# A hybrid attention and recurrence block: small-tile preparation beside attention, then a scan with batched solves beside the gates

## The chip, the core and the metric

The kernel runs on one core of one Trainium2 chip. The metric is the device time of one execution in microseconds; of several runs the median counts. One execution was taken by the hardware profiler; its span and rows are what is read below.

## What is computed

One layer over L = 1040 tokens (1024 and 16 meta tokens) of width 1024, batch 1, float32:

```python
hn = rms_norm(h, norm_mix)
q, k, v, f_logit, rw, gates = split(hn @ w_in)            # 3 x 512, 8, 1792, 2048
o_fox = forgetting attention: softmax(rms(q).rms(k)/8 + fcum[t] - fcum[s]) v, 8 heads of 64, causal
z = rw + mu * (shift(rw) - rw)                             # r, kr, vr: 512 each; zw, za, zg: 64, 64, 128
decay, a_rate, g = low-rank projections of zw, za, zg      # tanh, sigmoid
kk = kr * k_k / norm(kr * k_k)                             # per head
S_t = S_{t-1} diag(w_t) + (S_{t-1} a_t) b_t^T + v_t k_t^T; y_t = S_t r_t     # a = -kk, b = kk * a_rate
o_rwkv = (group_norm(y) + bonus) * g
merged = sigmoid(gates_1) * (o_fox @ w_bf) + sigmoid(gates_2) * (o_rwkv @ w_br)
h = h + merged @ w_o
h = h + (silu(conv(u_gate)) * conv(u_val)) @ ffn_down,  u = rms_norm(h, norm_ffn) @ ffn_up
```

The recurrence is computed in 17 chunks of 64 tokens. Within a chunk, the coupling of a token to the earlier ones is a strictly lower triangular 64 x 64 matrix a head, and (1 - A) has to be inverted: this inversion is called a solve here.

## The kernel before

All tensors lie with channels on partitions and tokens along the free axis. Large products run in three passes: weights and operands are split into float32r high and low parts, and `mm3` (L201 to L203) issues for each 128 x 128 weight tile the triple wh·xh, wh·xl, wl·xh. `wload` (L177) loads weights from DRAM through SP's queue (L185), rounds the high part on ACT (L188) and subtracts on POOL (L189). Small products are single float32 ones, for which the profile counts two passes each. Names: `mm`, `aux`, `tp`, `ch`, `gate`, `gn`, `t`, `s`, `o`, `rp` are PSUM tiles; names with `_d` lie in DRAM. Engines run in the order in which the program emits instructions, after a scheduler has interleaved the streams; DMAs issued on SP wait in SP's one queue.

Stage 1 (`stage1`, L259) does the first norm, in three chunks of tokens, then for each of four head pairs the preparation of the recurrence at the full width of 1040 tokens: projections (`rw_tile`), low-rank products (L304 to L313), cumulative decays, products `am` of a chunk's keys and queries (L394, stored to am_d L397), copies of the 32 x 32 diagonal blocks of these from DRAM to DRAM (`diags`, L404: a_d<-am_d, four a pair, runs of 128 bytes), transposes `bkt` (L411 to L415), and others. Stage 2 (`stage2`, L878) merges attention (`attention`, `q_block`) with the recurrence: `rw_pre` (L434) solves the systems of two chunks at a time, nine batches of 31 steps with two DVE operations each (L449, L451), `rw_chain` (L501) runs the 17 chunks, and `group_norm` (L847) follows at the end. The gates' projections, 384 triples, are a reserve: `fill` (L839) emits one to four triples at places where PE would wait, 84 of its steps right after stage 1. Stages 3 to 5 are the branches under the gates, the output projection with the second norm, and the MLP. `merge_streams` emits the steps of several generators in the order of virtual times that the `yield`s state.

```python
for k in range(2):                                   # diags, L401 to L404
    r = slice(32 * k, 32 * k + 32)
    for h in (2 * p, 2 * p + 1):
        nc.sync.dma_start(out=S.a_d[:, k, h], in_=S.am_d[:, r, h, r])
```

Of the kernel before, what the change touches and what calls it, by code (L numbers as in the profile page):

```python
# [7 lines left out]
F32 = mybir.dt.float32  # L8
F32R = mybir.dt.float32r
BF16 = mybir.dt.bfloat16  # L10
AF = mybir.ActivationFunctionType
# [26 lines left out]
CH = [(0, 346), (346, 692), (692, 1040)]  # L38
# [15 lines left out]
def constants(S):  # L54
    """The constants that the first products need."""
    nc, A, cp = S.nc, S.A, S.cp
    par = cp.tile([P, NPAR], F32, name="par")
    nc.sync.dma_start(out=par[:], in_=A["par"])
    S.par = lambda name, i=0: par[:, _PCOLS[name][0] + i:_PCOLS[name][0] + i + 1]
    S.pr = lambda name: par[:, _PCOLS[name][0]:_PCOLS[name][0] + _PCOLS[name][1]]  # L60
    S.ident = cp.tile([P, P], F32, name="ident")
    nc.sync.dma_start(out=S.ident[:], in_=A["ident"])
    S.ones = cp.tile([P, P], F32, name="ones")
    nc.vector.memset(S.ones[:], 1.0 / D)
    S.eps = cp.tile([P, 1], F32, name="eps")
    nc.vector.memset(S.eps[:], NORM_EPS)
    S.geps = cp.tile([P, 1], F32, name="geps")
    nc.vector.memset(S.geps[:], GN_EPS)
    S.wc = cp.tile([P, NCH, 4], F32, name="wc")


def constants2(S):
# [9 lines left out]
    S.a0h = lin("a0", 4, 0.5, 0.0)  # L82
    S.kah = lin("k_a", 4, 0.5, 0.0)
# [17 lines left out]
def stage0(S, p0):  # L101
    nc, tc = S.nc, S.tc
    S.w0 = []
# [7 lines left out]
    def tiles(*tags):  # L111
        r = []
        for t in tags:
            m = 6 if t[1:] in ("r_t", "k_t") else 3
            r.append(p0.tile([P, m, 348], F32, name="xt", tag=t))
        return r, [(i, j) for i, t in enumerate(r) for j in range(t.shape[1])][:KD]

    xs = []
    for c, (t0, t1) in enumerate(CH):
        n = t1 - t0  # L120
        tl, at = tiles(*(("zr", "zv", "sw"), ("tha", "inv", "ex"), ("ar_t", "cs"))[c])
        k = 0
        for t in tl:
            for j in range(0, t.shape[1], 3):
                m = min(3, KD - k)
                nc.sync.dma_start(out=t[:, j:j + m, :n], in_=S.A["xT"][:, k:k + m, t0:t1])
                k += m
                if k == KD:
                    break
        xs.append([tl[i][:, j] for i, j in at])  # L130
        if c == 0:
            constants(S)
        S.w0.append(wload(S, S.A["w_rw"][c], KD) if c < 2 else wload(S, S.A["w_rw"][c], KD, S.gp, "g", 1, 2))
    constants2(S)

    def stats(c):
        """1 / rms of a chunk's tokens, the same on all partitions."""
        n = CH[c][1] - CH[c][0]
        xt = xs[c]
        tl, at = tiles("bk_t", "kk")  # L140
        sq = [tl[i][:, j, :n] for i, j in at]
        na = 2
        for k in range(KD):
            with tc.issue_after(S.xhi[k].ins) if c == 1 else nullcontext():
                nc.scalar.activation(out=sq[k], in_=xt[k][:, :n], func=AF.Square)
                if k >= na:
                    nc.vector.tensor_tensor(out=sq[k % na], in0=sq[k % na], in1=sq[k], op=ALU.add)
        ps = psum(S, "aux")
        blk = [(0, 116), (116, 116), (n - 116, 116)]
        for j, (a, m) in enumerate(blk):  # L150
            for k in range(na):
                nc.tensor.matmul(ps[:m, j:j + 1], lhsT=sq[k][:, a:a + m], rhs=S.ones[:, 0:1], start=k == 0, stop=k == na - 1)
        r = p0.tile([P, 3], F32, name="r", bufs=2)
        nc.scalar.activation(out=r[:116], in_=ps[:116, 0:3], func=AF.Sqrt, bias=S.eps[:116])
        nc.vector.reciprocal(out=r[:116], in_=r[:116])
        ps = psum(S, "tp")
        for j, (a, m) in enumerate(blk):
            nc.tensor.matmul(ps[:, a:a + m], lhsT=r[:m, j:j + 1].broadcast_to([m, P]), rhs=S.ident[:m, :m], start=True, stop=True)
        return ps

    pss = [stats(0)]
    for c, (t0, t1) in enumerate(CH):
        ps = pss[c]
        n = t1 - t0
        xt = xs[c]
        for k in range(KD):
            nc.vector.scalar_tensor_tensor(out=xt[k][:, :n], in0=xt[k][:, :n], scalar=S.par("norm_mix", k),
                                           in1=ps[:, :n], op0=ALU.mult, op1=ALU.mult)
            S.xhi[k] = nc.scalar.copy(out=S.xh[k][:, 2 + t0:2 + t1], in_=xt[k][:, :n])  # L169
            nc.gpsimd.tensor_tensor(out=S.xl[k][:, 2 + t0:2 + t1], in0=xt[k][:, :n],  # L170
                                    in1=S.xh[k][:, 2 + t0:2 + t1], op=ALU.subtract)
        if c == 0:
            pss += [stats(1), stats(2)]
        yield c


def wload(S, src, kt, pool=None, tag="w", fb=3, wb=4):  # L177
    """Loads kt [128, 128] weight tiles and splits them into float32r high and low parts."""
# [3 lines left out]
    for h in range(0, kt, 4):  # L182
        n = min(4, kt - h)
        wf = pool.tile([P, 4, P], F32, name="wf", tag=tag + "f", bufs=fb)
        nc.sync.dma_start(out=wf[:, :n], in_=src[:, h:h + n])  # L185
        wh = pool.tile([P, 4, P], F32R, name="wh", tag=tag + "h", bufs=wb)
        wl = pool.tile([P, 4, P], F32R, name="wl", tag=tag + "l", bufs=wb)
# [7 lines left out]
def mm3(S, ps, w, x, first=True, last=True, mark=False):  # L195
    """Accumulates sum_k w_k^T x_k with hi/lo operand pairs."""
    nc = S.nc
    n = len(w)
    for k in range(n):
# [3 lines left out]
        ins = nc.tensor.matmul(ps, lhsT=wl, rhs=xh, start=False, stop=last and k == n - 1)  # L203
    if mark:
        S.last_pe = ins
# [6 lines left out]
def banks(S, **use):  # L212
    """Which PSUM slots each kind of product takes, in turn; S and M are slots of two banks."""
    S.psb = {k: v.split() for k, v in use.items()}
    S.psn = {k: 0 for k in use}
    S.half = {}


def slot(S, tag, name):
    w = 1024 if tag in "SM" else 512  # L220
    return (S.pf if tag == "f" else S.pp).tile([P, w], F32, name=name, tag=tag, bufs=1)


def psum(S, tag):
    """One bank; where a slot of two banks is named twice in a row, its halves in turn."""
# [19 lines left out]
def rw_tile(S, pool, mt, z, w, cs=range(3)):  # L245
# [3 lines left out]
    for t0, t1 in [CH[c] for c in cs]:  # L249
        n = t1 - t0  # L250
        ps = psum(S, "mm")
        mm3(S, ps[:, :n + 2], w, xwin(S, t0, n + 2), mark=True)
        t = pool.tile([P, 348], F32, name="zt", tag="zt", bufs=2)
        nc.scalar.activation(out=t[:, :n], in_=ps[:, 2:2 + n], func=AF.Identity, scale=mu1)
        nc.vector.scalar_tensor_tensor(out=z[:, t0:t1], in0=ps[:, 1:1 + n], scalar=mu, in1=t[:, :n],
                                       op0=ALU.mult, op1=ALU.add)


def stage1(S):  # L259
    nc, tc = S.nc, S.tc  # L260
    with tc.tile_pool(name="p1", bufs=1) as p1:
        T = lambda name, tag=None, bufs=1: p1.tile([P, LP], F32, name=name, tag=tag or name, bufs=bufs)
        mask = p1.tile([P, LP], BF16, name="smask")
        nc.gpsimd.memset(mask[:], 1.0)
        nc.gpsimd.memset(mask[:].rearrange("p (c t) -> p c t", t=64)[:, :, 0:1], 0.0)
        zs = [T("zs", "kf"), T("zs", "ei"), T("zk", bufs=2)]
        nc.gpsimd.memset(zs[2][:, L:LP], 0.0)
        tc.keep_in_program_order(nc.scalar.preload_act_table_set("sqrt_and_others"))
        for c in stage0(S, p1):
            for i in range(3):  # L270
                rw_tile(S, p1, i, zs[i], S.w0[i], [c])
        z = zs[0]
        t = T("th", "cs")
        nc.scalar.activation(out=t[:, :L], in_=z[:, :L], func=AF.Tanh, scale=0.5)
        nc.gpsimd.tensor_scalar(out=t[:, :L], in0=t[:, :L], scalar1=0.5, scalar2=0.5, op0=ALU.mult, op1=ALU.add)
        sgh, sgl = split(S, p1, t[:, :L], "sg", [P, L])
        z = zs[1]
        nc.scalar.activation(out=z[0:64, :L], in_=z[0:64, :L], func=AF.Tanh)
        wah, wal = split(S, p1, z[:, :L], "wa", [P, L])
        lup, gup = [S.wp.tile([P, 512], F32, name=n, tag="wf", bufs=3) for n in ("lup", "gup")]  # L280
        nc.sync.dma_start(out=lup[:], in_=S.A["lup"])
        nc.sync.dma_start(out=gup[:], in_=S.A["gup"])
# [914 lines left out]
```

## Time and profile before

| | |
|---|---|
| time, three runs | 2051.56, 2046.18, 2048.64 us; median 2048.64 |
| span of the profiled execution | 2045.7 us (its own time is not listed apart) |
| PE busy | 1879.8 us, 92% |
| DVE, ACT, POOL busy | 918.6 (45%), 751.7 (37%), 558.8 us (27%) |
| DMA | 167.95 MB, 82 GB/s |
| first norm (split of x on POOL) | 15.8 to 50.0 us |
| preparation's products am (L394) | 127.8 to 400.2 us |
| attention's scores (L745) | 499.4 to 1091.9 us |
| gates' products | 300.1 to 1098.3 us |
| stages 3 to 5 | the last 946 us |

A row of stretches gives, for a window of the span, the busy time of each engine with its number of instructions and the granted clock of TensorE (1.00 is full speed). A row of waits names the instruction that waited, what it waited for, the sum in us, how often, and the longest. A row of a group gives shape, count, busy us and mean ns of one, then the idle time just before and its cause.

### The profile page before, as it was taken

What the parts mean: (1) busy time and instruction counts of PE and PEld (TensorE: products, weight loads), DVE (VectorE), ACT (ScalarE), POOL (GpSimd) and SP (SyncE); (2) the same over time, 40 slices, a digit from 0 to 9 for tenths busy, and PEclk for the clock granted to TensorE, in tenths of its full rate; (3) what the DMA queues carried; (4) which work ended last, traced back from release to release, by engine and by line L of the source; (5) the groups of instructions that cost most, each with busy time, mean ns of one, the idle gap of its engine ahead of it and who ended that gap; (6) DMA issues with size and microseconds to landing.
All of it is one profiled execution on the core that took longest, in us unless ns stands there. A gap on an engine that the chain in (4) does not pass through costs nothing.

```text
span 2045.7 us, 32875 instructions
## 1 busy us (share of the span) xinstructions
PE 1879.8 (92%) x12812; PEld 1699.0 (83%) x12812; DVE 918.6 (45%) x2032; ACT 751.7 (37%) x1603; POOL 558.8 (27%) x552
## 2 busy tenths in 40 slices
PE   7996966747899999999899999999999999999999
PEld 6985855646778888888778999899998998999997
DVE  5264534128678642432764545733232332332333
ACT  5542332214333443443665434532232331322321
POOL 6421111103102211311431234533232332332322
PEclk9997979868999899999999999999999999999999
DMA  4233232541334332222223533211111111111112
GB/s 153 79 104 92 93 95 84 163 109 52 87 109 116 105 95 85 83 65 61 73 87 123 146 120 112 79 42 57 47 42 52 41 53 42 42 57 47 42 48 102
DMA packets 154483, 167.95 MB, mean 82 GB/s; under 512 B 47576, under 2 KB 111112, under 8 KB 154328
## 3 DMA queue, kind: packets, MB, share of 16 engines
q1 hardware_dynamic: 154072, 165.79, 27.0%
q8 instruction: 101, 1.65, 0.3%
q14 instruction: 54, 0.44, 0.1%
q0 software_dynamic: 256, 0.07, 0.0%
HBM read 123.39 MB, written 43.53 MB: 82 GB/s over the span
## 4 chain that ended last, share of the span: by engine, by line
PE 78%; DVE 7%; DMA 6%; SPq 4%; ACT 2%; issue 1%; POOL 0%; ACTq 0%; DVEq 0%; POOLq 0%
PE mm L202 14%; PE mm L201 14%; PE mm L203 14%; PE dn L201 4%; PE dn L203 4%; PE dn L202 4%; SPq L404 3%; PE gate L201 3%; PE gate L202 2%; PE gate L203 2%; PE t L780 2%; PE o L794 2%; PE am L394 2%; DVE x L451 1%; DVE xt L449 1%
## 5 line engine op out<-in xcount | busy, mean ns | idle before, releaser
L189 POOL TENSOR_TENSOR wl<-wf,wh 128x512 fp32r<-128x512 f32 (+1 forms) x268 | 352.6, 1319 | 787.3 <-ACT wh L188 738.2
L202 PE MATMUL mm<-x,wh 128*128 128x344 f32 (+1 forms) x1056 | 339.1, 321 | 0.0
L201 PE MATMUL mm<-x,wh 128*128 128x344 f32 (+1 forms) x1056 | 337.6, 320 | 1.1 <-DVE ug L1029 1.0
L203 PE MATMUL mm<-x,wl 128*128 128x344 f32 (+1 forms) x1056 | 337.4, 320 | 1.0 <-POOL wl L189 1.0
L188 ACT CAST wh<-wf 128x512 fp32r<-128x512 f32 (+1 forms) x268 | 163.7, 612 | 352.6 <-PE dn L202 182.4
L201 PE MATMUL mm<-xh,wh 128*128 128x348 f32 (+4 forms) x624 | 211.8, 341 | 3.6 <-ACT xh L169 1.6
L202 PE MATMUL mm<-xl,wh 128*128 128x348 f32 (+4 forms) x624 | 210.2, 337 | 0.7 <-POOL xl L170 0.7
L203 PE MATMUL mm<-xh,wl 128*128 128x348 f32 (+4 forms) x624 | 209.5, 336 | 0.0
L201 PEld LDWEIGHTS mm<-x,wh 128*128 128x128 f32 x1056 | 199.2, 189 | 1.9 <-ACT uv L1027 1.2
L203 PEld LDWEIGHTS mm<-x,wl 128*128 128x128 f32 x1056 | 199.0, 189 | 1.7 <-POOL wl L189 1.5
L202 PEld LDWEIGHTS mm<-x,wh 128*128 128x128 f32 x1056 | 199.3, 189 | 0.4
L201 PE MATMUL gate<-xh,wh 128*128 128x342 f32 x384 | 142.8, 372 | 2.9 <-ACT sg L834 2.9
L1056 DVE TENSOR_TENSOR h<-h,dn 128x512 f32<-128x512 f32 x96 | 66.0, 689 | 169.0 <-PE dn L203 168.4
L203 PE MATMUL dn<-gh,wl 128*128 128x512 f32 x352 | 138.8, 394 | 0.0
L201 PE MATMUL dn<-gh,wh 128*128 128x512 f32 x352 | 138.6, 394 | 0.0
L202 PE MATMUL dn<-gl,wh 128*128 128x512 f32 x352 | 138.6, 394 | 0.0
L201 PEld LDWEIGHTS mm<-xh,wh 128*128 128x128 f32 x624 | 121.9, 196 | 9.1 <-issue 4.1
L202 PEld LDWEIGHTS mm<-xl,wh 128*128 128x128 f32 x624 | 122.0, 196 | 5.9 <-issue 1.5
L202 PE MATMUL gate<-xl,wh 128*128 128x342 f32 x384 | 126.6, 330 | 0.0
L203 PE MATMUL gate<-xh,wl 128*128 128x342 f32 x384 | 126.2, 329 | 0.0
L203 PEld LDWEIGHTS mm<-xh,wl 128*128 128x128 f32 x624 | 121.8, 195 | 3.7 <-issue 1.0
L1028 DVE SCALAR_TENSOR_TENSOR uv<-mm,par,uv 128x342 f32<-128x342 f32 (+1 forms) x66 | 37.8, 573 | 162.4 <-ACT uv L1027 162.4
(313 smaller groups left out, 3704.2 us busy)
## 6 DMA issues: line engine op xcount, KB each, us to landing
wf<-in_w_up_dram SPq DMA_DIRECT2D x88, 256.0 KB
am<-am_d SPq DMA_DIRECT2D x17, 512.0 KB
sg_d<-sg SPq DMA_DIRECT2D x48, 171.0 KB
sg<-sg_d SPq DMA_DIRECT2D x48, 171.0 KB
wf<-in_w_gate_dram SPq DMA_DIRECT2D x32, 256.0 KB
wf<-in_w_out_dram SPq DMA_DIRECT2D x32, 256.0 KB
wf<-in_w_down_dram SPq DMA_DIRECT2D x32, 256.0 KB
wf<-in_w_rw_dram SPq DMA_DIRECT2D x28, 256.0 KB
```

The lines of the kernel that those rows point to most:

```text
L188: nc.scalar.copy(out=wh[:, :n], in_=wf[:, :n])
L189: nc.gpsimd.tensor_tensor(out=wl[:, :n], in0=wf[:, :n], in1=wh[:, :n], op=ALU.subtract)
L201: nc.tensor.matmul(ps, lhsT=wh, rhs=xh, start=first and k == 0, stop=False)
L202: nc.tensor.matmul(ps, lhsT=wh, rhs=xl, start=False, stop=False)
L203: ins = nc.tensor.matmul(ps, lhsT=wl, rhs=xh, start=False, stop=last and k == n - 1)
L394: nc.tensor.matmul(ps[:, j * P:(j + 1) * P], lhsT=bk_t[r, c0 + j, :], rhs=ar_t[r, c0 + j, :], start=True, stop=True)
L404: nc.sync.dma_start(out=S.a_d[:, k, h], in_=S.am_d[:, r, h, r])
L449: nc.vector.tensor_tensor(out=tv, in0=x[:, :ni, s:s + 1].broadcast_to([P, ni, m]), in1=la[:, s:s + 1, s + 1:s + 1 + m].broadcast_to([P, ni ...
L780: S.last_pe = nc.tensor.transpose(ps[:r, (2 * j + e) * 116:(2 * j + e) * 116 + nq], pb[e][i][:nq, k:k + r], S.ident[:nq, :nq])
L794: S.last_pe = nc.tensor.matmul(po[64 * e:64 * e + 64, :nq], lhsT=vt[:r, kb, 64 * e:64 * e + 64], rhs=pt[:r, 2 * j + e, :nq], start=kb == 0 ...
L1028: nc.vector.scalar_tensor_tensor(out=t[:, :n], in0=ps[:, 1:1 + n], scalar=cw(1), in1=t[:, :n], op0=ALU.mult, op1=ALU.add)
L1056: nc.vector.tensor_tensor(out=hs, in0=hs, in1=ps[:], op=ALU.add)
```

## The change

The first norm and the low-rank projections run per chunk of 384 tokens; the results of the latter go to DRAM (sw_d, tha_d, g_d), and their small products are single float32 ones. The preparation (`prep`) works on tiles of 384 tokens and is merged with attention from its start. There are no diagonal copies and no `fill`: the gates are emitted in whole tiles (24 products in a run, their Tanh on the way out of PSUM) once attention has ended, merged with the recurrence: `solve` for six chunks at a time (three batches; the systems are loaded straight from am_d, turned round by PE products with the identity, 30 steps of two DVE operations, turned back, stored to t_d), the chunks, and a group norm for each third of the tokens after chunks 5, 10 and 16. Sums of squares with their inverse square roots (`rsqrt_rows`) are made with products of one or two columns, tiny DVE operations on the rows and a broadcast by the identity, where before a product with a block matrix made them at full width. One ring of weight buffers serves all; a pair's queries are all made ahead of its blocks.

The core of the diff (removed parts of stage 1 and 2 cut):

```diff
-            def diags():
-                for k in range(2):
-                    r = slice(32 * k, 32 * k + 32)
-                    for h in (2 * p, 2 * p + 1):
-                        nc.sync.dma_start(out=S.a_d[:, k, h], in_=S.am_d[:, r, h, r])
...
+def solve(S, b):
+    nc, rp = S.nc, S.rp
+    cs = range(6 * b, min(6 * b + 6, NCH))
+    n = 8 * len(cs)
+    at = rp.tile([64, 48, 64], F32, name="at", bufs=1)
+    for j, c in enumerate(cs):
+        nc.sync.dma_start(out=at[:, 8 * j:8 * j + 8, :], in_=S.am_d[c, 0:64, :, 0:64])
+    x = rp.tile([P, 32, 32], F32, name="x", bufs=1)
+    for f in range(2):
+        ps = psum(S, "sv")
+        for t in range(16):
+            for k in range(2):
+                nc.tensor.matmul(ps[64 * k:64 * k + n, 32 * t:32 * t + 32], lhsT=at[:, :n, 32 * k + 16 * f + t],
+                                 rhs=S.ident[0:64, 32 * k:32 * k + 32], start=True, stop=True)
...
+    for s in range(1, 31):
+        m = 31 - s
+        tv = tmp[:nl, :s * m].rearrange("p (i t) -> p i t", i=s)
+        nc.vector.tensor_tensor(out=tv, in0=x[:nl, :s, s:s + 1].broadcast_to([nl, s, m]),
+                                in1=x[:nl, s:s + 1, s + 1:].broadcast_to([nl, s, m]), op=ALU.mult)
+        nc.vector.tensor_tensor(out=x[:nl, :s, s + 1:], in0=x[:nl, :s, s + 1:], in1=tv, op=ALU.add)
+        yield 0.8
...
+    for j, c in enumerate(cs):
+        nc.sync.dma_start(out=S.t_d[c], in_=at[:, 8 * j:8 * j + 8, :])
...
+def rsqrt_rows(S, pool, ps, sq, n, ind, w, eps=None, floor=None, ln=False):
...
+    for j in range(nb):
+        for i, q in enumerate(sq):
+            nc.tensor.matmul(ps[:m, o + w * j:o + w * j + w], lhsT=q[:, j * m:j * m + m], rhs=ind, start=i == 0, stop=i == len(sq) - 1)
...
+    else:
+        nc.vector.tensor_scalar(out=y.bitcast(I32), in0=v.bitcast(I32), scalar1=-0.5, scalar2=1597463007.0, op0=ALU.mult, op1=ALU.add)
+    for _ in range(1 if ln else 4):
+        nc.vector.tensor_tensor(out=t, in0=v, in1=y, op=ALU.mult)
+        nc.vector.scalar_tensor_tensor(out=t, in0=t, scalar=-0.5, in1=y, op0=ALU.mult, op1=ALU.mult)
+        nc.vector.scalar_tensor_tensor(out=y, in0=t, scalar=1.5, in1=y, op0=ALU.add, op1=ALU.mult)
+    for j in range(nb):
+        for i in range(w):
+            r = P // w
+            l = yt[:m, w * j + i:w * j + i + 1].broadcast_to([m, r])
+            nc.tensor.matmul(ps[i * r:(i + 1) * r, j * m:(j + 1) * m], lhsT=l, rhs=S.ident[:m, :m], start=True, stop=True)
...
 def gates(S):
-            for k in range(KD):
-                with S.tc.issue_after(S.last_pe.ins):
-                    mm3(S, ps[:, :342], w[k:k + 1], x[k:k + 1], first=k == 0, last=k == KD - 1)
+            mm3(S, ps[:, :342], w, xwin(S, t0 + 2, 342))
...
+    def rec():
+        yield from prep(S, p1)
...
+            yield from solve(S, 0)
+            nxt = iter(())
+            for c in range(NCH):
+                if c % 6 == 0:
+                    yield from nxt
+                    nxt = solve(S, c // 6 + 1) if c < 12 else iter(())
+                for t in rw_chain(S, c):
+                    yield t
+                    for _ in range(2):
+                        next(nxt, None)
+                if c in (5, 10, 16):
+                    yield from group_norm(S, (5, 10, 16).index(c))
...
+    for _ in merge_streams([(0.0, 1.0, att()), (0.0, 1.1, rec())]):
```

How the order moves. On SP, in the preparation of the first head pair before, between a weight load and the next ones:

```order
L185 DMA wf<-in_w_rw_dram 128x512
L397 DMA am_d<-am 128x2x256
L397 DMA am_d<-am 128x256
L404 DMA a_d<-am_d 17x32x32 x4
L415 DMA bkt_d<-bt 128x4x128 x2
L185 DMA wf<-in_w_rw_dram 128x512
L365 DMA ar_d<-ar_t 128x17x128
```

and after, in the same pair's first preparation tile, with attention's weights (in_w_qkv_dram) in the same queue:

```order
L394 DMA ar_d<-ar 128x6x128
L363 DMA tha<-tha_d 128x272
L404 DMA bon_d<-bon 128x384
L412 DMA v_d<-vt 128x3x128
L430 DMA am_d<-am 128x3x256
L437 DMA bkt_d<-bt 128x3x128
L430 DMA am_d<-am 128x3x256
L363 DMA sw<-sw_d 128x384
L437 DMA bkt_d<-bt 128x3x128
L199 DMA wf<-in_w_rw_dram 128x512
L199 DMA wf<-in_w_qkv_dram 128x512
```

The DRAM-to-DRAM copies are gone; the stores of a pair are spread over its tiles. On SP after, among the gates, the second set of solve loads (at) beside the first set's stores (t_d) and the loads of the chunks (tt, am, uv):

```order
L332 DMA t_d<-at 64x512 x4
L822 DMA sg_d<-sg 128x342
L199 DMA wf<-in_w_gate_dram 128x512
L276 DMA at<-am_d 64x8x64 x6
L822 DMA sg_d<-sg 128x342
L468 DMA tt<-t_d 64x512
L466 DMA am<-am_d 128x1024
L529 DMA y_d<-yt 128x4x64
L457 DMA uv<-v_d 64x512
L474 DMA bkt<-bkt_d 128x512
L199 DMA wf<-in_w_gate_dram 128x512
```

The solve loads stand ahead of the next gate weights. On PE before, around the products of a chunk, with attention (mm, t) and single gate triples between:

```order
L201 MATMUL mm<-xh,wh 128x348
L524 MATMUL ch<-pt,am 64x64 x3
L657 MATMUL t<-ident,v 128x128 x2
L657 MATMUL t<-ident,v 16x128
L524 MATMUL ch<-pt,am 64x64 x5
L201 MATMUL gate<-xh,wh 128x342
L202 MATMUL gate<-xl,wh 128x342
L203 MATMUL gate<-xh,wl 128x342
L202 MATMUL mm<-xl,wh 128x348
```

and on PE after, at the last gate triple; the rows after it belong to chunk 10, to the third solve (sv) and to chunk 11:

```order
L215 MATMUL gate<-xh,wh 128x342
L216 MATMUL gate<-xl,wh 128x342
L217 MATMUL gate<-xh,wl 128x342
L305 MATMUL sv<-ident,x 32x40 x16
L507 MATMUL ch<-uv,bkt 64x64 x8
L524 MATMUL ch<-ar,zb_7506 64x64
L525 MATMUL ch<-am,uv 64x64
```

From there to the first product of the branches 248 rows follow, all of chunks, solve and group norm; the last eight of them are the group norm's sums and broadcasts:

```order
L838 MATMUL gn<-y,bo_190 128x342
L599 MATMUL gn<-bo_190,sq 114x2 x3
L838 MATMUL gn<-y,bo_190 128x342
L622 MATMUL gn<-ident,ry 64x114 x6
L599 MATMUL gn<-bo_190,sq 114x2 x3
L622 MATMUL gn<-ident,ry 64x114 x6
L215 MATMUL mm<-orw,wh 128x342
```

Gate triples no longer stand between the products of the last six chunks.

More of the change, by code (lines that the diff above doesn't have):

```diff
@@ L134, in stage0 @@
[L134 to L142, printed above, removed]
-        for k in range(KD):
[L144 to L174, printed above, removed]
@@ L242, in split, with rw_tile @@
     return h, l
-def rw_tile(S, pool, mt, z, w, cs=range(3)):
+def rw_tile(S, mt, z, w, c, tag="mm"):
     nc = S.nc
     mu, mu1 = S.par("mu", mt), S.mu1[:, mt:mt + 1]
[L249 to L256, printed above, removed]
@@ L482, in rw_pre @@
-    for c, am in zip(cs, ams):
-        S.rw[c] = am
+            cp = nc.scalar.copy if (i + k) % 2 else nc.vector.tensor_copy
+            cp(out=at[r, :n, 32 * k + t0:32 * k + t0 + nt], in_=ps[r, :n * nt].rearrange("p (t c) -> p c t", c=n))
+        yield 1.5
+    hs = rp.tile([64, 48, 32], F32, name="hs", bufs=1)
+    nc.vector.transpose(out=hs[0:32, :n], in_=at[0:32, :n, 0:32])
+    for f in range(0, n, 16):
+        m = min(16, n - f)
+        ps = psum(S, "sv")
+        pv = ps.rearrange("p (h t) -> p h t", t=32)
+        for j in range(m):
+            nc.tensor.matmul(pv[32:64, j], lhsT=at[0:32, f + j, 32:64], rhs=hs[0:32, f + j], start=True, stop=True,
+                             tile_position=(0, 32))
+        nc.scalar.copy(out=hs[32:64, f:f + m], in_=pv[32:64, :m])
@@ new lines, in solve @@
+    yield 1.5
+    for f in range(0, n, 16):
+        m = min(16, n - f)
+        ps = psum(S, "sv")
+        pv = ps.rearrange("p (h t) -> p h t", t=32)
+        for j in range(m):
+            nc.tensor.matmul(pv[0:32, j], lhsT=hs[32:64, f + j], rhs=at[32:64, f + j, 32:64], start=True, stop=True,
+                             tile_position=(32, 0))
+        nc.scalar.copy(out=at[0:32, f:f + m, 32:64], in_=pv[0:32, :m])
+    for j, c in enumerate(cs):
+        nc.sync.dma_start(out=S.t_d[c], in_=at[:, 8 * j:8 * j + 8, :])
@@ L492, in rw_uv, with rw_am @@
     return uv, ar
+def rw_am(S, c):
+    am = S.rp.tile([P, 8, P], F32, name="am", bufs=2)
+    S.nc.sync.dma_start(out=am[:], in_=S.am_d[c])
+    tt = S.rp.tile([64, 8, 64], F32, name="tt", bufs=2)
+    S.nc.sync.dma_start(out=tt[:], in_=S.t_d[c])
+    return am, tt
 def rw_bkt(S, c):
@@ L883, in stage2, with stage12, att @@
+def stage12(S):
+    nc, tc = S.nc, S.tc
+    banks(S, mm="S S M M", st="t o", pr="A B", t="t", o="o")
+    p1_cm = tc.tile_pool(name="p1", bufs=1, side="right")
+    p1 = p1_cm.__enter__()
+    S.smask = p1.tile([P, 384], BF16, name="smask")
+    nc.gpsimd.memset(S.smask[:], 1.0)
+    nc.gpsimd.memset(S.smask[:].rearrange("p (c t) -> p c t", t=64)[:, :, 0:1], 0.0)
+    stage0(S)
+    banks(S, mm="S M")
+    S.op = None
     S.z = None
     S.ev = 0
-    def rwkv():
+    def att():
+        with tc.tile_pool(name="a", bufs=1) as ap:
+            forget(S, ap)
+            yield 12
+            S.q2 = [[ap.tile([66, 348], F32R, name=f"q2{i}{e}") for e in range(2)] for i in range(3)]
+            for i in range(3):
+                for e in range(2):
+                    nc.gpsimd.memset(S.q2[i][e][64:66, :].bitcast(F32), 1.0)
+            for p in range(NP_):
+                yield from attention(S, ap, p)
+        S.op_cm = tc.tile_pool(name="op", bufs=1)
+        S.op = S.op_cm.__enter__()
+        S.orw = [[S.op.tile([P, LT], F32R, name="orw", bufs=8) for _ in range(2)] for _ in range(4)]
+        banks(S, gate="S S M M", gn="t o", sv="t o", ch="A B")
+        yield from gates(S)
+    def rec():
+        yield from prep(S, p1)
+        p1_cm.__exit__(None, None, None)
+        while S.op is None:
+            yield 1.0
```

697 lines of the change are left out of this document (309 added, 388 removed).

## The prediction

> **What bounds the kernel now.** I read the busy time by stretch first, then the chain that ended last inside the weakest stretch, then the lines behind it. In the stretches the columns are length, busy us (instructions) of PE, PEld, DVE, ACT and POOL, the granted clock, DMA share and GB/s.
>
> ```profile
> 0.00:80.00 80.00, 65.58 (x375) 63.34 (x376) 31.26 (x60) 43.30 (x88) 51.87 (x82) 0.96 0.37 124
> 80.00:150.00 70.00, 70.00 (x429) 63.32 (x429) 39.37 (x53) 33.59 (x55) 19.53 (x21) 1.00 0.31 101
> 150.00:500.00 350.00, 242.85 (x1423) 210.10 (x1422) 142.31 (x279) 96.73 (x182) 63.22 (x67) 0.83 0.35 100
> 500.00:700.00 200.00, 183.67 (x1731) 156.72 (x1730) 154.84 (x585) 79.45 (x204) 33.51 (x35) 0.93 0.36 94
> 700.00:950.00 250.00, 245.39 (x2545) 208.94 (x2545) 89.17 (x224) 105.65 (x272) 45.52 (x46) 1.00 0.29 83
> 950.00:1100.00 150.00, 140.44 (x943) 116.34 (x943) 90.80 (x203) 85.36 (x214) 47.76 (x47) 0.95 0.24 72
> 1100.00:2045.70 945.70, 931.87 (x5376) 880.21 (x5374) 370.84 (x630) 307.60 (x590) 297.38 (x255) 1.00 0.22 69
> ```
>
> PE is the bound nearly everywhere, so the change is worth what it does to PE: its idle time, its clock, its work. From 1100 us on (branches, output, MLP) PE is full and the change leaves that code nearly alone: the whole question lies before 1100. There PE idles 107.1 + 16.3 + 4.6 + 9.6 = 137.6 us from 80 on, most of it in the preparation of the recurrence (150 to 500), at a clock of 0.83.
>
> ```profile
> 168.62 0.76 SPq L404
> 169.43 5.57 SPq L404
> 175.04 6.34 SPq L404
> 181.43 6.35 SPq L404
> 187.82 6.31 SPq L415
> 194.24 3.38 DMA bkt_d<-bt
> ```
>
> This piece of the chain (start, us, what) is SP's queue: the four diagonal copies a_d<-am_d of a head pair hold it some 25 us, the bkt stores stand behind them, and ACT's buffer bt behind those. All sixteen copies, ACT's wait for the stores, and PE's wait for ACT:
>
> ```profile
> L404 SPq DMA_DIRECT2D a_d<-am_d x16: 586/6021/6438, 168.6 to 417.4; - x16
>   DMA bkt_d<-bt: 75.6, 8
> PE tp L411 <- ACT bt L414: 36.1, 2, 18.9
> ```
>
> (First row: min/median/max ns.) Each stall also costs clock. Five stretches around the four copies and the first solve, columns as above:
>
> ```profile
> 180.60:207.90 27.30, 9.67 (x31) 8.26 (x32) 2.49 (x2) 5.75 (x10) 0.00 (x0) 0.50 0.44 119
> 272.70:293.20 20.50, 7.91 (x27) 7.09 (x28) 2.49 (x2) 3.51 (x8) 0.00 (x0) 0.50 0.54 149
> 347.80:375.10 27.30, 7.12 (x25) 6.36 (x26) 0.00 (x0) 2.36 (x5) 0.00 (x0) 0.50 0.47 128
> 419.50:450.20 30.70, 3.16 (x12) 3.16 (x13) 5.07 (x14) 0.97 (x2) 0.39 (x1) 0.50 0.55 120
> 487.80:501.50 13.70, 10.17 (x80) 7.41 (x80) 11.98 (x37) 6.98 (x16) 4.07 (x4) 0.50 0.07 15
> ```
>
> That is 119.5 us at exactly half clock with 38.0 us of PE work in it. From the first table, 2 x (1 - clock) x length gives 168 us at half clock in all; the other 48 us lie in short pieces that I count as busy, so half clock loses (38 + 48) / 2 = 43 us.
>
> **The change, part by part.** First the prices: PE by start times, two pieces of the chain (us for so many passes; one single float32 product is two passes), and a few groups (busy us, mean ns).
>
> ```profile
> 534.92 0.42 PE L768 MATMUL o<-ident,linv 116*64 116x116 f32 x4
> 535.27 0.69 PE L474 MATMUL rp<-hs,am 32*32 32x32 f32 x16
> 535.89 0.62 PE L794 MATMUL o<-apt,avt 128*64 128x116 f32 x8
> ...
> 738.57 1.14 PE L524 MATMUL ch<-pt,am 64*64 64x64 f32 x16
> 739.64 0.42 PE L201 MATMUL gate<-xh,wh 128*128 128x342 f32 x1
> 739.90 0.32 PE L202 MATMUL gate<-xl,wh 128*128 128x342 f32 x1
> 740.06 0.32 PE L203 MATMUL gate<-xh,wl 128*128 128x342 f32 x1
> ...
> 743.17 0.63 PE L533 MATMUL ch<-uv,bkt 128*64 128x64 f32 x16
> 743.74 0.42 PE L201 MATMUL gate<-xh,wh 128*128 128x342 f32 x1
> ```
>
> ```profile
> 23.16 0.92 PE aux L152 x10
> 156.74 1.36 PE aux L353 x4
> ```
>
> ```profile
> L752 DVE TENSOR_REDUCE nm<-mx 116x1 f32<-116x2 f32 x32 | 4.7, 150 | 0.5
> L869 DVE TENSOR_TENSOR y<-y,r 128x342 f32<-128x342 f32 x12 | 6.2, 513 | 0.2
> L541 DVE TENSOR_TENSOR zb<-ch,zb 64x256 f32<-64x256 f32 x30 | 12.6, 421 | 9.2 <-PE ch L533 8.8
> L542 DVE TENSOR_TENSOR zb<-zb,wc 64x256 f32<-64x256 f32 x30 | 13.8, 460 | 0.7
> ```
>
> 1. *The copies go and attention covers the preparation.* a_d and its sixteen issues vanish; preparation runs in small tiles between attention's products. Its stores (am_d, bkt_d, ar_d, v_d, bon_d) stay on SP, in smaller pieces with double buffers. I remove the 137.6 us of idle and put back: 15 us in the some 800 us where two streams cover each other (4.6 idle in 250 us of the like, 700 to 950); 8 us at attention's end, where softmax has little beside it (bounds 3 and 15); 5 us for the two later sets of solve loads; and the new open end. That end is in the order of PE: the last gate triple stands before chunk 11, so chunks 11 to 16 and the last two windows' group norms (the second runs between chunks) have no gates. A chunk's loop is 16 products (32 passes of 58 ns, between 743.17 and 743.74 sixteen take 0.57 in pairs and between 738.57 and 739.64 singly 1.07; I take 1.9), the copies pt and uv on ACT at an estimated 0.6 each (twice the width of zb in L541, which takes 0.42), 1.07, 0.57 and two halves of 421 + 460 ns on DVE: with semaphores 7.4 us, of which PE idles about 2, so 12 us for six. The group norm's chain per tile is a load, a product, and on DVE some 14 tiny operations (150 ns) and four wide ones (513 ns), about 9 us with ACT and POOL; two buffers of y make two rounds, and y must first reach DRAM and come back: 22 us (bounds 12 and 35). Stage 0 computes its square root in 13 tiny operations where ACT did it: +8 (0 to 15). Sum: -137.6 + 15 + 8 + 5 + 12 + 22 + 8 = -67.
>
> 2. *Clock.* Of the 43 us lost, stage 0's 3 stay (clock 0.96 up to 80). The open end is the question. The row from 487.8 holds the first solve and chunk at clock 0.50 although PE was busy 74% of it, and an open end like it would lose its whole 50 us of PE work again. The stretch from 700 to 950 holds chunks too, at 1.00. I take 11 us, the group norm's two rounds and what follows them, since a chunk leaves PE idle only some 2 us: -29 (bounds -40 and +10). The Trainium skill ("TensorE: Matmul & The Clock Gate", "Why this matters for your kernels") puts the limit at idle gaps of about 3 us between bursts of products. By that rule the chunks keep their clock and the sum stays at -29; by the row from 487.8 it would be +10, the rival (a) below. The stalls of 6 us above agree with the rule.
>
> 3. *Fewer changes of kind.* A float32 product beside a triple pays: the gate pass after ch starts its successor 0.26 later (739.64 to 739.90), the next 0.16 later. Counted in the order, PE changes between the kinds 602 times before and 443 after, since a gate tile is now one run of 24: 159 x 0.10 = -16.
>
> 4. *More work on PE.* The row-wise square roots add 185 products of one or two columns at 2 x 92 ns (0.92 for ten) = 34; their broadcasts 331 x 2 x 65 ns (0.35 from 534.92 to 535.27, less a change of kind, for four) = 43; the solves' transposes 384 passes of 32 columns at 39 ns (535.27 to 535.89: 0.62 for sixteen) and 384 of 40 to 48 at about 55 = 36; the small product of the low-rank projections as two passes of 0.34 instead of three of 0.16, and the rest, +9. Gone are the wide sums by a block matrix at 0.34 a pass (1.36 for four): queries and keys 48 passes = 16, kk 24 = 8, group norm 24 = 8, and the old sums of stage 0 and 4 with 7. Net +83. Low end: paired halves of the array overlap, as L533's did, +45; high end, 87 ns a broadcast, +115.
>
> 5. *At no cost, and its cover.* DVE's 526 solve operations become 180 of up to 240 elements, one after another; three solves of some 50 us each lie under attention's tail and gates, and if gates run out there PE waits for the solve itself. Gate weights now share one ring of three loads with all others; SP's issues of them stand behind at<-am_d and tt<-t_d. The gate's Tanh moves out of stage 3, whose ACT is a third busy. After 1100 I change nothing (2 either way).
>
> Sum: -67 - 29 - 16 + 83 = -29 us, a span of 2017. The median of the runs (2048.64) stands 2.9 above the profiled span (2045.7), so **2020 us**, 1.4% faster.
>
> **Rivals.** *(a) The open end falls to half clock.* If six chunks and the group norm (about 50 us of PE work) run as the row from 487.8 did, that work takes twice as long: +50, 2070, slower. It decides once the stretch from the last gate to the first product of the branches exceeds about 110 us (I have about 90). Against it stands the clock of 1.00 from 700 to 950.
>
> *(b) SP is blocked again.* at<-am_d reads 512 pieces of 256 bytes an issue, 17 issues. At L404's 6.0 us each, six hide behind attention and eleven stand among gate weights: 66 us less about 22 of weights loaded ahead, 2064, slower from about 3 us an issue on. Against it, the nearest loads into the core:
>
> ```profile
> L464 SPq DMA_DIRECT2D am<-t_d x34: 318/442/1274, 486.2 to 862.6; - x34
> ```
>
> 256 pieces of 128 bytes issue in 0.44 us, so 512 in an estimated 0.9. The Trainium skill ("DMA: Bandwidth & Descriptors", "Why a DMA increments its semaphore by 16 and not by 1") says that a transfer uses the largest number of engines up to 16 that divides the outermost sizes of both sides: one for L404's 17 chunks, 16 for the 64 rows of at. By that rule (b) is out; no row here names the engines of one transfer.
>
> *(c) The weight ring.* Three load buffers for everything; a wait of up to 2.0 us is on record:
>
> ```profile
> PE mm L203 <- POOL wl L189: 5.6, 7, 2.0
> ```
>
> At 2.0 us for each of some 24 weight sets of attention and preparation, +48: 2068. Against it: POOL was busy 63 of 350 us from 150 to 500, 18%.
>
> *(d) The new products overlap* in halves of the array: -38, 1982; with the open end at its low bound too (-10), about 1970.
>
> *(e) The stalls only move.* The merged streams cover each other as 500 to 700 did (16.3 idle in 200, so 8%): over half of the 800 us that is +25, 2045; over all of it +49, 2069.
>
> **How the numbers follow.** My forecast has 0.46, with its own range 1992 to 2045; (d) 0.17; (e) 0.14; (a) 0.11, (b) 0.06, (c) 0.06. Within 0.3% of before (2042.5 to 2054.8, about what a measurement of this kernel can tell from no change) lie 0.10 of (e) and 0.03 of the forecast; 0.02 of (e) lies on either side. Faster 0.43 + 0.17 + 0.02 = 0.62, same 0.13, slower 0.11 + 0.06 + 0.06 + 0.02 = 0.25. The range 1980 to 2068 leaves out half of (d) and half of (a), (b) and (c) together, 0.2.
>
> **What would show it.** Right: no idle of 6 us before 500 and a clock of 1.00 from 80 to the gates' end; PE's idle between 80 and the branches near 62 us, over half of it after the last gate; rows of the broadcasts near 65 ns a pass. Wrong: SP's at<-am_d over 3 us; a clock of 0.50 in the chunks after the last gate; PE waits for POOL's wl or ACT's wh above 20 us; broadcasts and one-column sums above 120 us in all.

## The result and the profile after

The changed kernel takes 2123.89 us (median of 2118.8 to 2127.53) against 2050.1 us (2046.18 to 2051.77) of the kernel before on the same chip: ratio 1.0362, interval 1.0342 to 1.0381. It is 3.6% slower where 1.4% faster was forecast. Its profiled span is 2125.7 us. Rows and accounts here are of one profiled execution of a kernel, which can lie up to 10 us from its median (2103.2 against 2093.83 in experiment 1, 2132.27 against 2123.35 in experiment 8). The stretches of the changed kernel, columns as before; I cut them where its preparation ends (665), where the first solve starts (777), at the last gate (1069) and at the first product of the branches (1179.2):

```profile
0.00:80.00 80.00, 55.85 (x236) 41.53 (x236) 37.50 (x90) 39.62 (x84) 38.25 (x75) 0.94 0.45 147
80.00:150.00 70.00, 62.80 (x313) 52.96 (x314) 13.99 (x22) 26.04 (x53) 16.33 (x29) 0.85 0.21 67
150.00:500.00 350.00, 338.17 (x2545) 299.26 (x2545) 159.84 (x407) 142.34 (x387) 78.34 (x98) 0.97 0.24 73
500.00:665.00 165.00, 155.51 (x1150) 132.82 (x1149) 81.85 (x209) 65.68 (x185) 31.64 (x43) 0.89 0.25 79
665.00:777.00 112.00, 91.98 (x582) 69.76 (x581) 38.82 (x107) 37.30 (x111) 14.40 (x17) 0.65 0.15 43
777.00:950.00 173.00, 172.58 (x2019) 164.75 (x2018) 62.73 (x149) 50.00 (x91) 28.13 (x27) 0.92 0.44 120
950.00:1069.00 119.00, 118.58 (x1246) 110.48 (x1245) 49.06 (x150) 35.60 (x66) 26.03 (x27) 0.99 0.47 137
1069.00:1179.20 110.20, 73.64 (x965) 62.13 (x964) 49.73 (x170) 30.90 (x62) 19.43 (x24) 0.69 0.52 148
1179.20:2125.70 946.50, 936.05 (x5412) 886.25 (x5412) 369.26 (x652) 272.82 (x519) 295.32 (x254) 1.00 0.21 64
```

From the branches on nothing changed (946.5 us; before, from 1098.8, 946.9). All 80 us lie ahead of them. The stalls of the preparation are gone: 338 of 350 us busy from 150 to 500. But two stretches with hardly a gate, attention's end (48 of the 1152 gate products, from 764 on) and the scan's open end (none but the last), ran at 0.65 and 0.69, and PE was busy 82% of the first.

To see what kind of time it is, I sum each product in the trace from its start to the next one's start, no longer than it ran; the rest is idle time. Products that start at half clock count half as work, and the other half as loss by the clock. Up to the first product of the branches, in us (rounded to 1 us; the some 10 us ahead of the first product are left out):

| kernel | branches start | work at full clock | lost to half clock | idle |
|---|---|---|---|---|
| before | 1098.8 | 904 | 42 | 143 |
| changed | 1179.2 | 958 | 111 | 101 |
| difference | +80 | +54 | +69 | -42 |

The idle time that the copies had caused was won. It was paid back once as work and more than once as clock. Four of the longest waits of PE in the changed kernel (sum, times, longest), the groups of the new small products, and the solve's loads:

```profile
PE gn L622 <- DVE ry L617: 14.7, 4, 6.6
PE st L599 <- DVE sq L141: 12.3, 2, 9.5
PE gn L838 <- DMA y<-y_d: 7.7, 3, 4.8
PE o L785 <- ACT apt L779: 6.0, 7, 1.6
```

```profile
L622 PE MATMUL o<-ident,ry 116*64 116x116 f32 x192 | 17.2, 321 | 1.5 <-DVE ry L617 1.5
L599 PE MATMUL o<-bo,sq 128*116 128x2 f32 x96 | 13.0, 251 | 0.9 <-DVE raw L637 0.9
```

```profile
L276 SPq DMA_DIRECT2D at<-am_d x17: 550/628/1767, 667.2 to 946.9; - x17
```

The group norm's rounds of tiny operations are the longest waits, as costed. The broadcasts shown take 90 ns a pass (17.2 us for 192), which looks like the high price of 87; but 72 of the 192 started at half clock. From start to start, the way my 65 was read, these took 117 ns and the other 120 took 63. SP is not blocked: an issue of at takes 0.63 us.

### The profile page after: what moved, and what is told of

Its sections match the earlier page's. It is cut to its first block, busy times and chain, and to the rows that moved or that the text cites. A ratio compares the mean times of both kernels' runs of the same rounds, so it can differ in the third digit from the quotient of the medians.

```text
span 2125.7 us, 36195 instructions
## 1 busy us (share of the span) xinstructions
PE 2005.2 (94%) x14452; PEld 1820.0 (86%) x14452; DVE 862.8 (41%) x1955; ACT 700.3 (33%) x1557; POOL 547.9 (26%) x591
## 5 line engine op out<-in xcount | busy, mean ns | idle before, releaser
L203 POOL TENSOR_TENSOR wl<-wf,wh 128x512 fp32r<-128x512 f32 (+1 forms) x268 | 344.4, 1287 | 778.7 <-ACT wh L202 722.3
L215 PE MATMUL gate<-xh,wh 128*128 128x342 f32 x384 | 128.1, 336 | 0.6 <-ACT sg L821 0.4
L215 PE MATMUL mm<-xh,wh 128*128 128x348 f32 (+5 forms) x336 | 116.6, 347 | 9.0 <-ACT sq L634 3.3
L216 PE MATMUL mm<-xl,wh 128*128 128x348 f32 (+5 forms) x336 | 116.1, 346 | 1.7 <-POOL xl L154 1.6
L217 PE MATMUL mm<-xh,wl 128*128 128x348 f32 (+5 forms) x336 | 113.7, 339 | 0.0
L1025 POOL TENSOR_TENSOR gl<-ug,gh 128x342 fp32r<-128x342 f32 (+1 forms) x66 | 58.2, 883 | 175.1 <-ACT gh L1024 175.1
L215 PE MATMUL pr<-xh,wh 128*128 128x386 f32 (+1 forms) x288 | 97.2, 338 | 0.5 <-DVE am L427 0.5
L750 ACT ACTIVATE pb<-s,nm 116x512 f32<-116x512 f32 (+11 forms) x112 | 63.3, 568 | 99.3 <-DVE nm L745 50.8
```

Source lines behind the costliest of these rows:

```text
L203: nc.gpsimd.tensor_tensor(out=wl[:, :n], in0=wf[:, :n], in1=wh[:, :n], op=ALU.subtract)
L215: nc.tensor.matmul(ps, lhsT=wh, rhs=xh, start=first and k == 0, stop=False)
L216: nc.tensor.matmul(ps, lhsT=wh, rhs=xl, start=False, stop=False)
L750: S.exp = nc.scalar.activation(out=o[:nq, o0:o0 + z - a], in_=ps, func=AF.Exp, bias=nm[:nq, e:e + 1], accum_out=ls[:nq, e, i:i + 1])
L1025: nc.gpsimd.tensor_tensor(out=gl[:, s], in0=g[:, :n], in1=gh[:, s], op=ALU.subtract)
```

## The experiments

Each experiment was measured beside the kernel before on its own chip, so its ratio is the safer number; the medians of the kernel before lie between 2046.25 and 2050.1 us. The theory after the comparison: the loss is mainly the clock, which falls where only narrow float32 products stand, in stretches that gates had filled before. Its rivals: the added work itself; and chains of softmax or scan that make PE wait, with the clock as a symptom.

**1. Preparation stretched along attention.**

```diff
-    for _ in merge_streams([(0.0, 1.0, att()), (0.0, 1.1, rec())]):
+    for _ in merge_streams([(0.0, 1.0, att()), (0.0, 1.4, rec())]):
...
-            yield 3.8        # gates
+            yield 4.84
```

> The changed kernel with the recurrence's stream merged at 1.4 instead of 1.1 (the preparation then ends nearly with attention, in the order of PE at row 2922 of 3078 instead of 2758 of 3084), and the gates' step 4.84 instead of 3.8, which keeps the later part as it was. Theory of the clock: attention's end (about 665 to 777 us) runs at half clock since only narrow float32 products stand there; with the preparation's products beside it, the half-clock time there falls by some 40 us and the kernel gains 15 to 35 us. Theory of the added work: the products are the same, so the time stays within 5 us. Theory of the softmax chain: attention's end waits for DVE and ACT, so filling the waits gains up to the idle time there, 10 to 15 us, and the clock is a symptom.

2093.83 us, ratio to before 1.0214 (1.019 to 1.0237): 30 us faster than the changed kernel. Work 958 as there, half-clock loss 92 (-19), idle 94 (-7). The added work cannot explain a gain without less of it; most of it is clock.

**2. Gates stretched along the scan.**

```diff
-            yield 3.8        # gates
+            yield 5.7
```

> The changed kernel with the gates' step 5.7 instead of 3.8: fewer gate tiles per chunk, so that the last one stands near the end of the last group norm (60 rows ahead of the branches instead of 248). Theory of the clock: the open end (1069 to 1179 us, clock 0.65 from 1100 on) gets wide products, its half-clock time of about 60 us falls below 20, and the kernel gains 30 to 50 us. Theory of the added work: the same products in another order, within 5 us. Theory of the chain's waits: the idle time of the open end (about 35 us) is filled, 25 to 35 us gained, with the clock following.

2119.99 us, 1.0351 (1.0303 to 1.0398): within the spread of the changed kernel, a miss for every theory that named a gain. The loss to the clock fell to 82 (-29), but the work rose to 977 (+19). Of this, 4 us are in the gates, whose runs are cut up among float32 products (42 more changes of kind), and 6 in the solves' products: one of 32 columns goes from 80 to 45 ns a pass at full clock in the probe below, not to 40, so the account makes their work at half clock too small. The rest is not explained. The stretch from the last gate (1113) to the branches (1166) stayed open, at 0.62 and more than half idle:

```profile
1113.00:1166.00 53.00, 23.36 (x212) 17.39 (x211) 21.61 (x80) 13.58 (x28) 9.96 (x11) 0.62 0.42 123
```

The 60 rows that stand there in the order of PE take 53 us: rows say nothing of how long the last group norm's chain takes.

**3. Gates in attention's end.** After the preparation `rec` runs gate tiles until attention has ended; these leave PSUM without their Tanh, which the branches then apply.

```diff
...
-        while S.op is None:
-            yield 1.0
+        with tc.tile_pool(name="eg", bufs=1, side="right") as S.eg:
+            banks(S, gate="A B")
+            while S.op is None:
+                yield next(S.gates)
```

> The changed kernel with about ten gate tiles run while attention's end runs alone (after the last preparation tile), in the two banks that are free then; their Tanh moves back to the branches. Theory of the clock: attention's end keeps a clock near 1.00 (now 0.60 from 700 to 750) and loses some 40 us of its length beyond the gates' own time; the chunks, which have fewer gates then, get a longer open end at half clock, which gives 15 to 25 us back: 15 to 25 us faster in all. Theory of the added work: within 5 us. Theory of the softmax chain: the 10 to 15 us of idle time there are filled, and as many more come back at the open end: no change.

2114.17 us, 1.0315 (1.0278 to 1.0351): 10 us faster by the medians, though the runs overlap (up to 2121.70 here, from 2118.80 in the changed kernel). In the account the loss to the clock is 84 (-28), with work 961 and idle time 105, some 4 more of each. Attention's end now ran near full clock, with 7 us idle instead of 20; the scan's open end, with fewer gates left, ran at 0.77 and was idle for 49 us instead of 37:

```profile
665.00:777.00 112.00, 104.86 (x756) 93.19 (x754) 29.50 (x85) 43.30 (x109) 26.24 (x26) 0.92 0.29 86
1000.00:1159.00 159.00, 109.83 (x1638) 93.25 (x1637) 88.07 (x299) 47.24 (x94) 27.01 (x35) 0.77 0.51 148
```

**4. The kernel before with its copies turned.**

```diff
-nc.sync.dma_start(out=S.a_d[:, k, h], in_=S.am_d[:, r, h, r])
+nc.sync.dma_start(out=S.a_d[:, k, h].rearrange("c s t -> s c t"),
+                  in_=S.am_d[:, r, h, r].rearrange("c s t -> s c t"))
```

> The kernel before with one edit: the diagonal copies a_d<-am_d go with the 32 rows as the outermost size and the 17 chunks second, the same 544 pieces of 128 bytes. By the rule of the Trainium skill (one engine for 17, 16 for 32) each issue falls from 6.0 us to about 0.6, the stalls in the preparation and their half clock go, and the kernel takes 1960 to 2000 us. If the pieces from DRAM to DRAM are what is slow, the issue stays near 6 us and the time near 2050. A third case: the issues shorten but the queue's other stores take their place, 2020 to 2040.

1961.41 us, 0.9568 (0.9546 to 0.959): 87 us faster than before, by one line. The copies, and the stretch of the preparation:

```profile
L404 SPq DMA_DIRECT2D a_d<-am_d x16: 547/631/1393, 166.7 to 335.6; - x16
```

```profile
150.00:400.00 250.00, 225.78 (x1359) 198.54 (x1359) 135.17 (x261) 91.54 (x170) 59.55 (x63) 0.97 0.49 141
```

0.63 us an issue instead of 6.02. Work stays at 904, the loss to the clock goes from 42 to 36 and the idle time from 143 to 60. The stalls whose removal was the changed kernel's largest expected gain did not need its new order.

**5. Wide sums of queries and keys in the changed kernel.**

```diff
-    rsqrt_rows(S, ap, pm, [sq], n, S.bo64[:, 0:P:64], 2, eps=NORM_EPS, ln=True)
+    nc.tensor.matmul(pm[:, :n], lhsT=S.bo64[:], rhs=sq[:, :n], start=True, stop=True)
+    ... Ln, Exp at full width, a Newton step for keys
```

> The changed kernel with the sums of squares of queries and keys as before: one wide product with the block matrix, Ln and Exp at full width on ACT (and a Newton step at full width for keys), in place of the one- and two-column products and broadcasts. Those take 41 us of PE in the changed kernel (23 at full clock, 18 at half), the wide form about 24 at half the instructions. Theory of the added work: 15 to 25 us faster. Theory of the clock: the places that drop to half clock stay (attention's end has none of these sums in its last part), so 5 to 15 us faster. If DVE and ACT bind attention, the wide form costs them time: 0 to 10 us slower.

2082.14 us, 1.0144 (1.01 to 1.0188): 42 us faster, more than any theory gave. Work 936 (-22), as the theory of the work said; loss to the clock 96 (-15) and idle 93 (-8) come on top. The row-wise form was dearer twice: in passes, and in clock.

**6. A probe: PE alone.** Appended behind the end of the changed kernel, operands in place (the narrow ones read the identity), one PSUM bank, no other engine; the edit in short:

```diff
+    wide(80); narrow(400)                      # 64 x 48 weights, 32 columns, float32
+    wide(80); 140 products 116 x 116 x 116
+    wide(80); 150 products 128 x 116, 2 columns
+    wide(80); 10 x (narrow(16); wide(3, 342))
+    wide(80); 6 x (narrow(48); wide(3, 342))
+    wide(80); 70 wide products of 66 rows
```

> The changed kernel with a stretch of PE work appended after its end, whose results are not used; no other engine takes part, so PE has no reason to wait. Parts, each behind 80 products of 128 x 512 in float32r: 400 float32 products of 64 x 48 weights and 32 columns; 140 of 116 x 116; 150 with two columns; ten times 16 of the first kind and 3 wide ones of 342 columns; six times 48 and 3; at the end 70 wide ones with 66 rows. Theory A (narrow products count as idle for the clock): the first and third part fall to 0.50 within some 7 us, the mixed ones stay at 1.00. Theory B (only idle time of PE counts): all parts stay at 1.00, and what falls in the kernel falls through waits.

```profile
2142.60:2202.20 59.60, 59.60 (x802) 59.50 (x801) 0.00 (x0) 0.00 (x0) 0.00 (x0) 0.55 0.01 2
2222.90:2251.30 28.40, 28.40 (x280) 28.35 (x279) 0.00 (x0) 0.00 (x0) 0.00 (x0) 1.00 0.00 1
2270.10:2323.70 53.60, 53.60 (x302) 53.60 (x300) 0.00 (x0) 0.00 (x0) 0.00 (x0) 0.54 0.00 1
2345.10:2377.40 32.30, 32.30 (x351) 28.91 (x351) 0.00 (x0) 0.00 (x0) 0.00 (x0) 0.63 0.01 2
2397.70:2448.70 51.00, 51.00 (x596) 48.79 (x596) 0.00 (x0) 0.00 (x0) 0.00 (x0) 0.53 0.01 1
```

PE never waited. The clock (0.55, 1.00, 0.54, 0.63, 0.53) fell 5 to 6 us into the two parts of 32 and of 2 columns alone, and 8 and 3 us into the two mixtures; it stayed at 1.00 for 116 columns, and for the wide products of 66 rows at the end. Theory B, that only waits count, is out, and so is A's hope for thin mixtures: three wide products in every 2.2 us, 30% of the time, did not hold it.

**7. Gates spread over all that follows the preparation** (one tile per 7.0 steps in attention's end, per 6.4 beside the scan).

> The changed kernel with its 48 gate tiles spread over all that follows the preparation: one per 7.0 steps while attention's end runs, then one per 6.4 steps beside the scan, so that the last one stands 99 rows ahead of the branches. Theory of the clock: both stretches at half clock lose most of it, half-clock time falls from 270 to below 150 us and the kernel is 35 to 60 us faster than the changed one (2065 to 2090). Theory of the added work: within 5 us of the changed kernel. If wide products only help where they are dense, the clock stays low in the thin mixture: 5 to 20 us faster.

2105.51 us, 1.0291 (1.0261 to 1.0322): 18 us faster, the third case. The clock lost 80 (-31), at the price of work 972 (+14), as in 2.

**8. Added products, results unused, in attention's end.**

```diff
...
+            if S.extra:        # preparation has ended
+                px = psum(S, "xt")
+                with S.tc.issue_after(mo.ins):
+                    for x in (S.xh[0], S.xl[0], S.xh[1]) * 2:
+                        nc.tensor.matmul(px[:, :342], lhsT=S.xh[2][:, 2:130], rhs=x[:, 2:344], start=True, stop=True)
```

> The changed kernel with 156 more wide products whose results are not used, six after each group of transposed weights in attention's end: 156 x 0.158 = 25 us of added PE work at full clock. Theory of the clock: attention's end runs near 1.00 instead of 0.60, which is worth more than the added work: 5 to 25 us faster. Theory of the added work: 25 us slower. Theory of the softmax chain (PE waits there anyway): the products fill idle time, 0 to 10 us slower.

2123.35 us, 1.0379 (1.0352 to 1.0406): no change against 2123.89, though the work rose by 31 us (989). The loss to the clock fell by 21 (90), idle time by 7 (94). So it was not waits that took the products in, but mostly the clock that they held. Attention's end, now to 787, ran at 0.89 instead of 0.65:

```profile
665.00:787.00 122.00, 105.72 (x781) 87.14 (x778) 44.09 (x118) 40.47 (x119) 18.26 (x20) 0.89 0.16 48
```

It is no gain, as the theory of the clock had hoped, but the pure theory of work (25 us slower) falls.

**9. The kernel before, copies split into 16 chunks and 1.**

```diff
-nc.sync.dma_start(out=S.a_d[:, k, h], in_=S.am_d[:, r, h, r])
+nc.sync.dma_start(out=S.a_d[0:16, k, h], in_=S.am_d[0:16, r, h, r])
+ ... chunk 16 alone, rows outermost
```

> The kernel before with one edit: each diagonal copy a_d<-am_d of 17 chunks is split into one of 16 chunks and one of the last chunk alone (rows outermost); the order of the pieces in the large part stays that of before. If it was the 17 that kept the copies on few engines, the issue of the large part falls from 6.0 to about 0.6 us and the kernel takes 1955 to 1975 us, as with the rows outermost (1961). If the order of the pieces made the difference there, the large part still takes near 6 us and the time stays above 2030.

1968.93 us, 0.9607 (0.9591 to 0.9623). The part of 16 chunks, with its pieces in the old order:

```profile
L404 SPq DMA_DIRECT2D a_d<-am_d x16: 534/621/1308, 161.1 to 332.4; - x16
```

So it was the 17, not the order of the pieces. The Trainium skill ("DMA: Bandwidth & Descriptors", "Why a DMA increments its semaphore by 16 and not by 1") says that a transfer takes the largest number of engines up to 16 that divides the outermost sizes: both edits agree with it, at 6.02 us for 17 and 0.62 and 0.63 for 16 and 32. No record names the engine, but the packets of the trace fit: the 2176 pieces of the first pair's four copies lie over 25.2 us in the kernel before, with never more than two under way at a time, and over 3.4 us in experiment 4, with 8.7 on average.

**10. Edits of 5, 1 (at 1.3) and 7 (one tile per 7.5 steps beside the scan) together in the changed kernel.**

> The changed kernel with three edits together: the wide sums of queries and keys (alone 42 us faster), the slower preparation (at 1.3; at 1.4 alone 30 us faster) and the gates spread over all that follows the preparation (alone 18 us faster). If the three save at different places, 2035 to 2055, no slower than the kernel before; if they all save the same half-clock time, 2060 to 2085. Either way it stays above 1961, the kernel before with its copies mended, since it keeps about 30 us more PE work.

2064.46 us, 1.0076 (1.0056 to 1.0096): 59 us of the 90 that they gave singly, so they share part of the lost clock, and still slower than before. Work 951, clock 75, idle 83.

**11. The mended kernel before with a smaller block of gates** (`fill(S, 56)` for `fill(S, 84)`).

> The kernel before with the mended copies (rows outermost, 1961 us) and 56 instead of 84 steps of the gate reserve in a block after the preparation, so that some 30 triples more are left for the places where the solves and attention make PE wait. Theory of the clock: the stretch of the solves (400 to 610, clock 0.89, 16 us idle) gains, 1945 to 1958. If the reserve already lasts, the block only moves: 1957 to 1965. If the start of the scan needs the block to cover the first solve: 1965 to 1980.

1979.84 us, 0.9665 (0.9646 to 0.9685), 18 us slower than with 84. The work up to the branches fell from 904 to 890 us and 17 us more of it came behind: the places left over did not take the reserve in. 84 stays the better number.

**12. A second probe**, the edit again in short.

```diff
+    for k, m, n, cnt in ((64, 64, 64, 300), (128, 64, 64, 250), (128, 64, 116, 150), (64, 128, 128, 150),
+                         (116, 64, 116, 150), (32, 32, 32, 400), (128, 48, 32, 300), (128, 128, 64, 250)):
+        wide(80); cnt products of k x m weights and n columns
+    wide(80); 14 x (narrow(16); wide(9, 342))
```

> As the first probe, a stretch of PE work appended to the changed kernel, its results unused; each part stands behind 80 wide products. Float32 products by weights' rows x columns and moving columns: 64 x 64 with 64 (the chunks'), 128 x 64 with 64, 128 x 64 with 116 (attention's output), 64 x 128 with 128 (am), 116 x 64 with 116 (broadcasts), 32 x 32 with 32, 128 x 48 with 32, 128 x 128 with 64; at the end fourteen times 16 of 64 x 48 with 32 and 9 wide ones of 342. If the moving columns decide, those with 116 and 128 stay at 1.00 and those with 32 and 64 fall to 0.50; if the part of the array in use decides, 64 x 64, 32 x 32 and 128 x 48 fall and 128 x 128 with 64 stays. The last mixture, wide for over half its time, stays at 1.00 if a share decides.

```profile
2136.40:2171.60 35.20, 35.20 (x602) 35.10 (x601) 0.00 (x0) 0.00 (x0) 0.00 (x0) 1.00 0.01 2
...
2388.70:2429.80 41.10, 41.10 (x802) 41.04 (x801) 0.00 (x0) 0.00 (x0) 0.00 (x0) 0.53 0.01 3
2451.30:2478.40 27.10, 27.10 (x602) 27.06 (x601) 0.00 (x0) 0.00 (x0) 0.00 (x0) 1.00 0.01 3
...
2571.70:2616.00 44.30, 44.24 (x575) 40.69 (x574) 0.02 (x1) 0.00 (x0) 0.00 (x0) 1.00 0.01 1
```

Shown are 64 x 64 with 64 columns, 32 x 32 with 32, 128 x 48 with 32, and the mixture that is wide for half its time. Only 32 x 32 fell; neither rule that I had written down holds alone. Rows of weights times moving columns, per ns of a pass, sorts the parts of one kind in both probes: 128 x 32 in 45 ns (91) and 64 x 64 in 59 ns (70) held the clock, 64 x 32 in 49 ns (42) lost it. It is no rule for mixtures: three wide products of 342 columns and 32 passes of 64 x 32 in 2.22 us come to 89, and lost it. Multiplying by the columns of the weights as well sorts the parts just as well, so the measure stays open. In these shapes, dense chunk products, transposes, attention's output and broadcasts do not by themselves lower the clock; sums in two columns and the solves' products of 32 do.

## Why the prediction was wrong

**The step that failed is item 2, the clock.** It gave -29 us and weighed, as the other bound, the row from 487.8; the account shows +69. I reckoned lost clock as something that the stalls cause and that goes with them, plus 11 us at the open end. In fact half clock rose from 171 to 270 us, and by the clock of the stretches only 68 of it lie in the open end (2 x 0.31 x 110.2); 78 lie in attention's end, and the other 120 in the stretches ahead of it and in the scan. Rival (a) had the mechanism (its sign, an open end of over about 110 us, came at 110.2), but for one place only.

What lowers the clock there I counted in the trace, in windows of 3.413 us, the step in which the granted clock changes, over the changed kernel and experiments 1 to 3. Where triples filled 40% of a window at full clock, it fell behind 0 of 696. With fewer triples and PE busy below 70%, it fell behind 49 of 67; with PE busy longer, behind 27 of 301. Sixteen of these 27 windows PE filled to 96% or more, with 39 to 82 of the solves' small products in each: there narrow products brought the clock down inside the kernel, without waits, as in the probe. And it comes back slowly: from half clock, 24 of 194 windows with under 5% of triples were followed by full clock, against 41 of 51 with 40% or more. Where nothing wide stands between them, waits that add up to a third of a window were mostly followed by a fall; whether wide products would have held the clock through such waits these counts can't say, since none of the 696 windows had PE busy below 70%. I had taken the Trainium skill's rule ("TensorE: Matmul & The Clock Gate", "Why this matters for your kernels") of gaps over some 3 us as support for -29 and for the low chance of rival (a). This case differs: none of the changed kernel's 19 falls after its first 40 us had a gap above 3.1 us in the three windows ahead, and the probe's had none at all. The kernel before, with `fill` between the narrow products, ran 700 to 950 at 1.00; that was worth more than I gave it, since I costed the gates' new place only by the waits that they cover.

**Item 1, idle time: -67 forecast, -42 measured.** The open end came as said (36.6 us idle against 34). Two terms were mis-sized: attention's end, 8 us with bounds 3 and 15, against 20 us in a stretch of 112; and the time in which two streams cover each other, 15 us, against 28.5 from 80 to 665 alone (7.2, 11.8 and 9.5 in the three stretches).

**Items 3 and 4, work: +67 forecast, +54 measured**, right within the bounds. The largest terms came as priced: from start to start the row-wise sums and broadcasts took 94 us of PE, 76 with half clock counted half as in the account, where I had 77 (their groups, L599 and L622, add up to 105 us busy). The other terms were not measured one by one. What I had not asked for is the second price of these products, the clock: of what experiment 5 saved, 22 us were work, 15 clock and 8 idle time.

**Rivals.** (b) fell as argued, at 0.63 us an issue; (c) did not show (3.0 us of waits for wl in all). Of (d) at most a part came: the work lies 13 us under the forecast where (d) asked for 38. Of (e) a part came: the 28.5 us above, where (e) at its lesser price had 15 + 25. That a stall is gone says nothing about what takes its place in the sum: a forecast of -1.4% was the difference of two large terms, and the range was too narrow for that.

What is not settled: how much of the half clock in attention's end comes from its short waits and how much from its narrow products, since every edit there changed both. No run took the waits away alone, and the sixteen windows of solves all lie at its very end or behind it. Nor is it known which property of a narrow product lowers the clock.

## What to carry to other kernels

Look for the cheapest cure of a stall before a new order of the work: one form of transfer, issued sixteen times with an outermost size of 17, cost 87 us, and turning two of its axes brought them back. Price independent wide products by the clock they hold, not only by the waits they fill, and try to keep some in every stretch of narrow products and short waits, to its very end. It is no gift: spread thinly they came with 14 to 19 us more work (experiments 2 and 7), and products added for the clock alone won nothing (8). A reduction in fewer columns may spare DVE and ACT, but on PE a product of two columns took as long as one of 116 in the probe (102 and 101 ns a pass at full clock), and a dense run of them lowered the clock.

## What the runs showed of the hardware

A dense run of float32 products can itself bring the clock to one half: 150 of two columns took 179 ns a pass (53.6 us for 300), against the 92 ns of the kernel before, 400 of 64 x 48 with 32 columns 74 ns a pass on average against 49 in the mixtures at full clock. Products of 116 columns at 101 ns held 1.00. A mixture held it with wide products for half the time and lost it with 30%. These are single runs, their narrow operands mostly zeros; the sixteen windows of solves show the same fall on the kernel's own data.
